# A third permanent buffer for raw weights, squares written elsewhere, and a new order, in a two-layer encoder on one core

## The chip, the cores and the metric

The kernel runs on one core of one Trainium2 chip, as one launch. The metric is the device time of that launch in microseconds. The time before is 1423.53 us, the median of three runs (1422.23 to 1426.47).

## The reference

The reference is a two-layer encoder trunk over 512 tokens of width 1024, all in float32. Each layer does

```
x = x + post_norm(mixer(pre_norm(x)))
x = x + post_norm(swiglu(pre_norm(x)))     # swiglu(h) = (silu(h @ w_gate) * (h @ w_up)) @ w_down
```

with RMS norms, `y = x / sqrt(mean(x*x) + 1e-6) * g`. The mixer of layer 0 is neighbourhood attention on an 8 x 64 grid (16 heads of 64, a window of 8 x 16 with a learned position bias); the mixer of layer 1 is a mixture of three dilated sliding-window attentions, (window, dilation) = (128, 1), (512, 4), (2048, 16), whose outputs are weighted by their softmax denominators. Each mixer ends in a projection by a 1024 x 1024 matrix. The channel mixer has a hidden width of 2816, that is 22 blocks of 128. The output is the stream x, 512 x 1024.

## The kernel before

The engines are called PE (TensorE, the matrix engine), DVE (VectorE), ACT (ScalarE), POOL (GpSimd) and SP (SyncE, which issues most transfers). Each works through its own row of instructions in order and waits on semaphores for the others.

**Products.** A float32 product is made of three products of a shorter format. Each operand is split into a high part, which ACT copies (L219), and a remainder, which DVE subtracts (L220); then `mm3` (L234 to L236) multiplies high by high, high by low and low by high into one bank of PSUM, the matrix engine's output memory. So every weight is loaded raw by a transfer, split by ACT and DVE into a slot of `wring`, and then multiplied. The large products of a layer are computed by a scheme with seven products of half-size blocks in place of eight; it needs sums of blocks of the weights. For gate, up and the mixers these sums are made on POOL and DVE from the raw weights in place (class `Seven`, L302 to L308). For down they are made beforehand in DRAM by POOL's transfers, some of which accumulate (tensor `wsum`, L749), and which stand between POOL's other instructions during the gate/up stage.

**Stages of a layer.** The mixer; then `out_proj`, which multiplies four blocks of 128 tokens (products 0 to 3, banks `yo`), applies the post-norm (`postnorm_half`, L506 and L507: a Square with a running sum on ACT, a multiply by the gain on DVE; `postnorm_sum`, L440 to L513), the next pre-norm (L438, L449), and turns the result by transposes on PE (`tr_o`, L465), which ACT and DVE empty into split operands (L456, L459); then `gate_up`, 22 units of one block of 128 hidden columns each, 84 matmuls 256 wide per unit; then `down`, seven products over the hidden blocks in pieces of two (matmuls 512 wide, banks `yd_pp` and `yd_s`), the last of which ends in the post-norm of token blocks 2 and 3 (`end`).

**Raw weights.** The pool `wpool` has a tag `raw` with two permanent buffers of 2 x 1024 floats per partition. In `gate_up` an arena `more` of six halves, a ring of three more buffers, stands beside them; the arena lies where operands of the mixer (`rxb`) were, so it can be loaded only after `out_proj` has ended. Of five units in a row the first two use permanent buffers (`f % 5 < 2`), the others the ring. `down` uses the same memory as a ring of ten halves, four of permanent buffers and six of the arena. Its first loads go to the permanent halves (in the profile `r_d`, issued at L779; gate/up weights there are `r_gu`, those in the arena `raw`).

**What sets the order.** Nothing is left to a scheduler: `TURNS`, a compressed table of numbers, holds for each engine the order in which the recorded instructions are to stand; `in_order` reads it and chains them.

**Scratch.** The program reserves memory in each partition for the descriptors of POOL's own transfers; by default 16 KB.

## Time and profile before

| | |
|---|---|
| median of the runs | 1423.53 us |
| profiled execution | 1423.35 us |
| span of its trace | 1421.6 us |
| mean granted clock of TensorE | 0.995 |
| busy: PE, DVE, ACT, POOL | 98%, 83%, 64%, 38% of the span |
| bytes moved | 253.21 MB, 178 GB/s |

The profile is of one execution; 1.75 us of it lie outside the span. A row of its timeline gives the start in us, the duration, the engine, the source line, the operation with its output and input tiles, how often it follows itself, and in brackets the idle time of that engine before the row and what ended it. "PEld" is the loading of weights into the matrix engine, which runs beside the matmuls. "SPq" and "POOLq" mark rows that issue transfers; such a row lasts as long as its queue was held, and the landing is given apart. Stretches list busy time by engine, the clock granted to TensorE (1.00 is full speed), the busy share of the DMA engines and what they moved. By stage: start 0 to 20, mixer of layer 0 to about 200, its `out_proj` to about 240, `gate_up` to 460, `down` to 560, the mixer of layer 1 to about 1050, `out_proj` to 1090, `gate_up` to 1310, `down` to the end.

### The profile page before, as it was taken

What the parts mean: (1) busy time and instruction counts of PE and PEld (TensorE: products, weight loads), DVE (VectorE), ACT (ScalarE), POOL (GpSimd) and SP (SyncE); (2) the same over time, 40 slices, a digit from 0 to 9 for tenths busy, and PEclk for the clock granted to TensorE, in tenths of its full rate; (3) what the DMA queues carried; (4) which work ended last, traced back from release to release, by engine and by line L of the source; (5) the groups of instructions that cost most, each with busy time, mean ns of one, the idle gap of its engine ahead of it and who ended that gap; (6) DMA issues with size and microseconds to landing.
All of it is one profiled execution on the core that took longest, in us unless ns stands there. A gap on an engine that the chain in (4) does not pass through costs nothing.

```text
span 1421.6 us, 27828 instructions
## 1 busy us (share of the span) xinstructions
PE 1387.5 (98%) x10714; PEld 1298.9 (91%) x10714; DVE 1181.7 (83%) x1891; ACT 914.0 (64%) x1853; POOL 541.5 (38%) x394
## 2 busy tenths in 40 slices
PE   8999999999999999999999999999999999999997
PEld 8989978999998888999999999999888999999886
DVE  7699969998887888997578887877748898897886
ACT  7489965555554767744467787888766555555674
...
GB/s 261 100 192 199 176 305 247 218 221 292 266 224 273 201 224 178 161 158 179 120 114 102 119 173 98 143 110 81 249 208 158 90 120 199 177 106 171 194 221 96
DMA packets 86645, 253.21 MB, mean 178 GB/s; under 512 B 19312, under 2 KB 31600, under 8 KB 84464
## 3 DMA queue, kind: packets, MB, share of 16 engines
...
## 4 chain that ended last, share of the span: by engine, by line
PE 78%; DVE 9%; ACT 6%; DMA 3%; issue 2%; POOL 1%; SPq 0%; POOLq 0%; DVEq 0%; ACTq 0%
PE gu L234 9%; PE gu L236 9%; PE gu L235 9%; PE pp_d L234 4%; PE pp_d L235 3%; PE pp_d L236 3%; DVE wring L220 3%; PE yd_s L235 3%; PE yd_s L234 3%; PE yd_s L236 3%; PE yd_pp L234 2%; PE yo L234 2%; PE yd_pp L235 2%; PE yd_pp L236 2%; PE yo L235 2%
## 5 line engine op out<-in xcount | busy, mean ns | idle before, releaser
L234 PE MATMUL gu<-rxa,wring 128*128 128x256 f32 x704 | 193.9, 280 | 0.7 <-DVE memc L715 0.3
L236 PE MATMUL gu<-rxa,wring 128*128 128x256 f32 x704 | 191.7, 278 | 1.9 <-DVE wring L220 1.9
L235 PE MATMUL gu<-rxa,wring 128*128 128x256 f32 x704 | 193.0, 277 | 0.0
L220 DVE TENSOR_TENSOR wring<-r_d,wring 128x1024 fp32r<-128x1024 f32 x112 | 142.6, 1280 | 38.9 <-ACT wring L219 38.5
L220 DVE TENSOR_TENSOR wring<-raw,wring 128x1024 fp32r<-128x1024 f32 (+1 forms) x120 | 152.0, 1276 | 16.6 <-ACT wring L219 15.3
L219 ACT ACTIVATE wring<-raw 128x1024 fp32r<-128x1024 f32 (+1 forms) x120 | 122.2, 1021 | 63.1 <-PE gu L235 36.5
L219 ACT ACTIVATE wring<-r_d 128x1024 fp32r<-128x1024 f32 x112 | 115.6, 1041 | 34.0 <-POOL r_d L304 6.4
L234 PEld LDWEIGHTS gu<-rxa,wring 128*128 128x128 f32 x704 | 131.6, 188 | 3.1 <-DVE mem L715 1.1
L236 PEld LDWEIGHTS gu<-rxa,wring 128*128 128x128 f32 x704 | 130.9, 188 | 3.0 <-DVE wring L220 2.5
L235 PEld LDWEIGHTS gu<-rxa,wring 128*128 128x128 f32 x704 | 132.2, 188 | 0.2
L234 PE MATMUL pp_d<-rxa,wring 128*128 128x256 f32 x384 | 107.4, 283 | 1.0 <-DVE mem L558 1.0
L442 POOL TENSOR_TENSOR rs_yd<-v_yd,consts 128x1 f32<-128x1 f32 x8 | 8.9, 1112 | 257.7 <-DVE v_yd L440 257.7
L235 PE MATMUL pp_d<-rxa,wring 128*128 128x256 f32 x384 | 106.1, 280 | 0.0
L236 PE MATMUL pp_d<-rxa,wring 128*128 128x256 f32 x384 | 105.0, 279 | 0.0
L235 PE MATMUL gu<-rxc,wring 128*128 128x256 f32 x352 | 98.1, 280 | 1.5 <-DVE rxc L459 1.5
L234 PE MATMUL gu<-rxc,wring 128*128 128x256 f32 x352 | 98.3, 282 | 0.5 <-ACT rxc L456 0.5
L236 PE MATMUL gu<-rxc,wring 128*128 128x256 f32 x352 | 97.8, 280 | 0.6 <-DVE wring L220 0.6
L219 ACT ACTIVATE rxc<-mem 128x512 fp32r<-128x512 f32 (+2 forms) x95 | 60.5, 644 | 51.3 <-PE yd_s L235 24.3
L302 POOL TENSOR_TENSOR raw<-raw 128x512 f32<-128x512 f32 x24 | 44.0, 1835 | 122.6 <-DVE wring L220 102.3
L219 ACT ACTIVATE wring<-r_gu 128x1024 fp32r<-128x1024 f32 x60 | 63.6, 1060 | 42.1 <-PE gu L235 19.3
L220 DVE TENSOR_TENSOR wring<-r_gu,wring 128x1024 fp32r<-128x1024 f32 x60 | 83.2, 1387 | 7.3 <-ACT wring L219 7.1
L220 DVE TENSOR_TENSOR rxc<-mem,rxc 128x512 fp32r<-128x512 f32 (+2 forms) x92 | 70.9, 777 | 14.1 <-ACT rxc L219 11.7
...
## 6 DMA issues: line engine op xcount, KB each, us to landing
wsum<-wd POOLq DMA_DIRECT2D x24, 1408.0 KB, 11.8
r_d<-dil_qk SPq DMA_DIRECT2D x48, 512.0 KB, 4.3
raw<-wg SPq DMA_DIRECT2D x24, 512.0 KB, 5.1
raw<-wu SPq DMA_DIRECT2D x24, 512.0 KB, 7.1
wsum<-wsum POOLq DMA_DIRECT2D x8, 1408.0 KB, 7.8
raw<-wsum SPq DMA_DIRECT2D x22, 512.0 KB, 4.4
r_gu<-wg SPq DMA_DIRECT2D x20, 512.0 KB, 5.5
r_gu<-wu SPq DMA_DIRECT2D x20, 512.0 KB, 5.9
```

The lines of the kernel that those rows point to most:

```text
L219: act.activation(h, src, AF.Copy)
L220: dve.tensor_sub(l, src, h.bitcast(F32))
L234: i = pe.matmul(o, s[0], m[0], start=start, stop=False, skip_group_check=True)
L235: pe.matmul(o, s[0], m[1], start=False, stop=False, skip_group_check=True)
L236: pe.matmul(o, s[1], m[0], start=False, stop=stop, skip_group_check=True)
L302: self.added = e[0].tensor_add(q[0], q[0], q[2])
L442: pool.tensor_tensor(r, v, mhalf, op=ALU.pow)
```

## The change

No operation is added or removed on any engine; what changes is where things stand, in memory and in each engine's row.

- The scratch for descriptors is 4 KB in place of 16. In the 12 KB set free lies a third permanent `raw` buffer (8 KB). In `gate_up`, three of six units in a row now use permanent buffers (`f % 6 < 3`), so units 0, 1, 2 may be loaded before the arena is there, where before 0 and 1 could, and units 18, 19 and 20 are the last in permanent buffers, where before 20 and 21 were. `down` has a ring of twelve halves in place of ten.
- The Square of a post-norm half no longer writes the place that the multiply then overwrites: in `out_proj` it writes the next block's buffer, in `end` a part of operands that are done with.
- In `down`'s last pass the last three pieces, not two, are kept until the others are done; they are then multiplied for token block 2 first and block 3 after.
- `TURNS` is new. Its text tells nothing; the rows of the engines show it below.

The diff, without `TURNS` (source lines after the table stand one line later than before, from `out_proj` on up to four):

```diff
@@ -210,7 +211,7 @@
 
     def load2(srcs, name, raw=None):
         if raw is None:
-            raw = tagged(wpool, [P, 2 * D], F32, "raw", f"r_{name}", 2)
+            raw = tagged(wpool, [P, 2 * D], F32, "raw", f"r_{name}", 3)
         for i in range(2):
             nc.sync.dma_start(raw[:, i * D:(i + 1) * D], srcs[i])
         return raw
@@ -501,9 +502,9 @@
             for i, v in ((D1, d1), (S2, s2), (S3, h1a), (S4, h1b)):
                 put(i, v)
 
-    def postnorm_half(hf, sq, y, g, name):
+    def postnorm_half(hf, sq, y, g, name, squares=None):
         m, s = small(f"ym{hf}_{name}"), slice(hf * 512, hf * 512 + 512)
-        act.activation(sq[:, s], y, AF.Square, scale=1.0 / 32.0, accum_out=m)
+        act.activation(sq[:, s] if squares is None else squares, y, AF.Square, scale=1.0 / 32.0, accum_out=m)
         dve.tensor_mul(sq[:, s], y, g[:, s])
         return m
 
@@ -512,8 +513,8 @@
         for s in ([slice(0, 512), slice(512, 1024)] if halves else [ALL]):
             dve.scalar_tensor_tensor(x[:, s], sq[:, s], r, x[:, s], op0=ALU.mult, op1=ALU.add)
 
-    def postnorm(sq, y, g, x, name):
-        postnorm_sum(sq, [postnorm_half(hf, sq, y[hf], g, name) for hf in range(2)], x, name)
+    def postnorm(sq, y, g, x, name, squares=(None, None)):
+        postnorm_sum(sq, [postnorm_half(hf, sq, y[hf], g, name, squares[hf]) for hf in range(2)], x, name)
 
     def v_quarter(vt, srcs, name, raw=None):
         u = units2(srcs, name, raw=raw, at=0)
@@ -646,7 +647,7 @@
         g1 = gain(gains[0], a["g_mix_post"][layer])
         g2 = gain(gains[1], a["g_ffn_pre"][layer])
         us = [u for k in range(0, KD, 2) for u in units2(w[k:k + 2], f"wo{k}_{layer}", us[k:k + 2])]
-        hs = {}
+        hs = {0: next(rhn)}
 
         def product(t):
             y = [bank(("pp", "pp", "s", "s", "pp", "o", "pp", "pp")[2 * t + hf], f"yo{layer}_{t}_{hf}")
@@ -658,9 +659,12 @@
             return y
 
         def post(t, y):
-            x, hs[t] = next(rbig), next(rhn)
+            x = next(rbig)
             load_x(x, t)
-            postnorm(hs[t], y, g1, x, f"o{layer}_{t}")
+            if t < NT - 1:
+                hs[t + 1] = next(rhn)
+            postnorm(hs[t], y, g1, x, f"o{layer}_{t}",
+                     (hs[t + 1][:, :512], hs[t + 1][:, 512:]) if t < NT - 1 else (None, None))
             nc.sync.dma_start(spill[2 * layer][t], x)
             xs_[t] = x
 
@@ -700,7 +704,7 @@
         def unit_of(f):
             if f in units or f >= FT:
                 return units.get(f)
-            raw = load2((wg[layer, f], wu[layer, f]), f"gu{layer}_{f}", None if f % 5 < 2 else next(raws))
+            raw = load2((wg[layer, f], wu[layer, f]), f"gu{layer}_{f}", None if f % 6 < 3 else next(raws))
             b, g = bank(("s", "s", "pp", "o", "pp", "pp")[f % 6], f"gu{layer}_{f}"), next(g_)
 
             def sink(n, left, other):
@@ -761,7 +765,7 @@
         x1a, x1b, x2a, x2b = (hm[:, i * QF:(i + 1) * QF] for i in range(4))
         pieces = [slice(2 * i, min(2 * i + 2, FT // 2)) for i in range(FT // 4 + 1)]
         last = len(pieces) - 1
-        raws = [tagged(wpool, [P, 2 * D], F32, "raw", f"r_d{layer}{i}", 2) for i in range(2)]
+        raws = [tagged(wpool, [P, 2 * D], F32, "raw", f"r_d{layer}{i}", 3) for i in range(3)]
         raws = [r[:, i * D:i * D + D] for i in range(2) for r in raws]
         raw_ = cycle(raws + [more[:, i * D:i * D + D] for i in range(6)])
         ga, gb, ua, ub = (a["wd"][layer, i] for i in range(4))
@@ -858,7 +862,7 @@
             kept = []
             for i, w in enumerate(loaded(uab if n == 0 else every)):
                 ops = operands2(xp((x1a, x2b)[n], i), w, f"{nm}{('s3', 'x2b')[n]}_{i}")
-                if i > last - 2:
+                if i > last - (3 if n else 2):
                     kept.append(ops)
                 else:
                     prod(left, ops)
@@ -877,7 +881,7 @@
                 prod(left, ops, False, (m,))
 
         def end():
-            m0 = [postnorm_half(0, hs[t], left[t - 2], gp, f"d{layer}_{t}") for t in (2, 3)]
+            m0 = [postnorm_half(0, hs[t], left[t - 2], gp, f"d{layer}_{t}", xp(x2b, t - 2)) for t in (2, 3)]
             for t in (2, 3):
                 postnorm_sum(hs[t], (m0[t - 2], ms[t - 2]), xts[t], f"d{layer}_{t}", layer == 1 and t == NT - 1)
                 out_of(t)
@@ -1395,7 +1399,7 @@
               .reshape(2, 4, P, 2 * QF),
     }
     arrays = {n: np.ascontiguousarray(v) for n, v in arrays.items()}
-    nc = bacc.Bacc("TRN2", target_bir_lowering=False, num_devices=1)
+    nc = bacc.Bacc("TRN2", target_bir_lowering=False, num_devices=1, dynamic_dma_scratch_size=4096)
     aps = {n: nc.dram_tensor(n, v.shape, mybir.dt.from_np(v.dtype), kind="ExternalInput").ap()
            for n, v in arrays.items()}
     out = nc.dram_tensor("out", (NT, P, D), F32, kind="ExternalOutput").ap()
```

What the new order does is shown at three places. A number behind a name tells apart tiles of one name; it differs between the two programs.

The first place is the end of `gate_up` in layer 0, on PE: `yd_pp` is the first product of `down`, `gu_18` to `gu_21` are units of gate/up. Before:

```order
L234 MATMUL gu_21_4872<-rxa,wring 128x256
L235 MATMUL gu_21_4872<-rxa,wring 128x256
L236 MATMUL gu_21_4872<-rxa,wring 128x256
L234 MATMUL yd_pp_5193<-wring,rxc 128x512
L234 MATMUL yd_pp_5194<-wring,rxc 128x512
L234 MATMUL gu_20_4762<-rxa,wring 128x256
```

and now:

```order
L235 MATMUL yd_pp_5195<-wring,rxc 128x512
L235 MATMUL yd_pp_5196<-wring,rxc 128x512
L235 MATMUL gu_19_4655<-rxa,rxc 128x256
L236 MATMUL gu_19_4655<-rxa,rxc 128x256
L237 MATMUL gu_19_4655<-rxa,rxc 128x256
```

The first matmuls of `down` stood among the last two units, with 48 matmuls of gate/up behind them; they now stand among units 18 to 20, with 132 behind them. What feeds them is a split on DVE. Its row from the last split of unit 18 (`r_gu_18`) to the first of the down weights (`r_d`) is now:

```order
L221 TENSOR_TENSOR wring<-r_gu_18_4542,wring 128x1024
L309 TENSOR_TENSOR r_gu_19_4652<-r_gu_19_4652 128x512
L816 TENSOR_TENSOR mem<-mem 128x512
L221 TENSOR_TENSOR wring<-r_gu_19_4652,wring 128x1024 x2
L717 TENSOR_TENSOR memc_2767<-memc_2767,gu_18_4545 128x256
L221 TENSOR_TENSOR vbig<-r_gu_20_4762,vbig 128x512
L305 TENSOR_TENSOR r_gu_20_4762<-r_gu_20_4762 128x512
L309 TENSOR_TENSOR r_gu_20_4762<-r_gu_20_4762 128x512
L723 TENSOR_TENSOR mem<-memc_2767,mem 128x2x256
L719 TENSOR_TENSOR memc_2767<-mem,gu_18_4545 128x256
L221 TENSOR_TENSOR wring<-r_gu_20_4762,wring 128x1024
```

with five more rows (a sum, a memset and three splits of 512) before `wring<-r_d`. Before, the buffer came free with unit 20, and from its last split to that of `r_d` 15 rows of the same kinds stood between. On SP, six loads into the arena stood right ahead of the first load of `r_d`; now there are three.

The second place is the end of `out_proj` in layer 1, on PE. `yo_3` is the product of token block 3, `tr_o_0` and `tr_o_1` are the transposes of blocks 0 and 1. Before:

```order
L465 MATMUL tr_o_0_0_11762<-ident,mem 128x128 x4
L236 MATMUL yo_3_0_11856<-rxb_5993,rxa 128x512
L234 MATMUL yo_3_1_11857<-rxb_5993,rxa 128x512
L235 MATMUL yo_3_1_11857<-rxb_5993,rxa 128x512
L236 MATMUL yo_3_1_11857<-rxb_5993,rxa 128x512
L465 MATMUL tr_o_0_1_11769<-ident,mem 128x128 x4
L465 MATMUL tr_o_1_0_11776<-ident,mem 128x128 x4
L465 MATMUL tr_o_1_1_11783<-ident,mem 128x128 x4
L234 MATMUL gu_0_12014<-rxc,wring 128x256
```

and now, at the first of them and at the third:

```order
L236 MATMUL yo_3_1_11860<-vbig,rxa 128x512
L466 MATMUL tr_o_0_0_11765<-ident,mem 128x128 x4
L466 MATMUL tr_o_0_1_11772<-ident,mem 128x128 x2
L237 MATMUL yo_3_1_11860<-wm_11591,rxa 128x512
L235 MATMUL yo_3_0_11859<-rxa 128x512
L236 MATMUL yo_3_0_11859<-rxa 128x512
```

```order
L235 MATMUL yo_3_0_11859<-rxb_5996,rxa 128x512
L236 MATMUL yo_3_0_11859<-rxb_5996,rxa 128x512
L237 MATMUL yo_3_0_11859<-rxb_5996,rxa 128x512
L466 MATMUL tr_o_1_0_11779<-ident,mem 128x128 x4
L466 MATMUL tr_o_0_1_11772<-ident,mem 128x128 x2
L236 MATMUL yo_3_1_11860<-rxb_5996,rxa 128x512
```

Four products stood between the first group and the three that end the stage; now 25 products follow the first group and 14 the group `tr_o_1_0`, and the last of these groups stands behind 14 matmuls of units 2 and 0. On DVE the norms of blocks 0, 1 and 2 are now taken one after the other; before, block 1's came first, and half of block 2's (`yo_2_0`) before block 0's:

```order
L507 TENSOR_TENSOR mem<-yo_1_1_11677,mem 128x512
L507 TENSOR_TENSOR mem<-yo_1_0_11676,mem 128x512
L513 SCALAR_TENSOR_TENSOR mem<-mem,consts 128x1024
L507 TENSOR_TENSOR mem<-yo_2_0_11790,mem 128x512
L507 TENSOR_TENSOR mem<-yo_0_0_11626,mem 128x512
```

In layer 0's `out_proj` the first transpose moves up likewise: it stood at the end of product 3 and now stands behind the first four matmuls of it.

The third place is the end of the program, on DVE, with what each row waits for. Before:

```order
L507 TENSOR_TENSOR mem<-yd_s_14435,mem 128x512 [waits Activation_49]
L440 TENSOR_SCALAR v_yd_2_15193<-ym_d_2_15187,ym_d_2_15162 128x1
L507 TENSOR_TENSOR memc_12005<-yd_s_14436,mem 128x512 [waits Activation_49]
L440 TENSOR_SCALAR v_yd_3_15199<-ym_d_3_15190,ym_d_3_15165 128x1
L513 SCALAR_TENSOR_TENSOR mem<-mem,rs_yd_2_15195 128x1024 [waits DMAHW3_49,Pool_49]
```

and now:

```order
L508 TENSOR_TENSOR mem<-yd_s_14440,mem 128x512 [waits Activation_49]
L441 TENSOR_SCALAR v_yd_2_15199<-ym_d_2_15193,ym_d_2_15156 128x1
L508 TENSOR_TENSOR memc_12008<-yd_s_14441,mem 128x512 [waits Activation_49]
L441 TENSOR_SCALAR v_yd_3_15205<-ym_d_3_15196,ym_d_3_15159 128x1
L514 SCALAR_TENSOR_TENSOR mem<-mem,rs_yd_2_15201 128x1024 [waits DMAHW3_49,Pool_49]
```

`L507`/`L508` is the multiply of a post-norm half. Its order and its wait for ScalarE ("Activation") are the same in both.

More of the change, by code (lines that the diff above doesn't have):

```diff
@@ new lines @@
+    "SDA~+gP1tnFl?4s!r*cQOq^J1A&W$RZZPrHd+yEq02j0zln>wBbg*B-E&bsK`|`>-B4B~>3j@Bt1I*0K+@7&GWT5_4ZscdcO$SlY_yq=6-;U1W"
+    "`ybQ>@WV#&G%B#>;BJ8#2X_SY?#RJ)16fn8HCijW{+WQAzbHs5ZV~(q==`g;kqBB_d;Z+*>8QZ-=g;YsgGYGx!Gj0=`+bWm4vLoF0QA4Ab~}~k"
+    "&$85PZ4qq<9CqS4zd&!_05e|$-1XC^W(eq+xa{j8u;5@QxaPp~NRcyXgS<fWqxw-1(`L&77<_%b;O^z+<#h+k20yoOIG<-smyB8{R#kA-;(`NI"
+    "I5*fH3<g{^&sX!@WiCics}%yHkxOCIQC`BC5SjJeu_8_-8JC#tqsUpnyZ7$h1NYn`sp7Pk=QpF9q*>6YRk5CB)XmL*R{Z%F`H-$NXz|jeOP3A~"
+    "4lW5Oym+ZY-p=ms{?1Nv;R4i5G5y5U{6$GUp(-u$G%#(97~;+Yny$EeJ*+g85>~yt)LrZ@bRA$3imL(j`w)e^fgV>!Q`|^e0}p|xcK+uN&I`E5"
@@ new lines @@
+    "NhF>D6RY*O)$#_kHXzB+qybmOaAE~6X)#4qhsUGOu`c;QMAu93j&B4X@3cI~nQHr*B^OlN(mKS*)fxtQs@TxseA7kRMJ<hL!bhm1L=T)5c3@>N"
+    "ocD1R$*4Vuc^C(A8_OI+fOG^(<$(e__G6akN*KYUJr?s)V5>(gxhJ?#%@QNIP!0iw$|)I%n1B;};)2u<R1&HgexxE54x=Gthk6}MAtQ}fK+k~Z"
+    "$?_^Q#)p}%kZ1d;q}&R(_ByVVlV}I?rq)JRa0_1LyI?WIVo=<RQP81O66xHjyft9j6Z4lClSS>5IDsDb((iV25#ZC*?vPF3@(5<c9H>r5LA;dN"
+    "Li59LK?TgvqrQ}M=uG*{Us7Qp7RMwj!CA>#TI{9yQ7BJoh=)0zGS_7prsK8Sag2f?8#Z%(CMDA*L>$`RH$9qm(lzDzm|Z{%U?|_8g?M2aMNCM="
+    "Mk4pV1@31-S9FQ!;_DEc5G%XjBYxMXp(G9Kfpi@<fEk}}@Vr(#Bk+9?x45|DdkM5b2Es*hvL?Wr5fo`cQO<W!pxW&&`Uv<DCX%pn>U2oQN@XBp"
```

97 lines of the change are left out of this document (44 added, 53 removed).

## The prediction

> **What bounds the kernel now.** I read the page's overview first, then the chain of waits, then TensorE's own waits, and last the stretches in which those waits lie.
>
> ```profile
> PE 1387.5 (98%) x10714; PEld 1298.9 (91%) x10714; DVE 1181.7 (83%) x1891; ACT 914.0 (64%) x1853; POOL 541.5 (38%) x394
> PE 78%; DVE 9%; ACT 6%; DMA 3%; issue 2%; POOL 1%; SPq 0%; POOLq 0%; DVEq 0%; ACTq 0%
> 300.00:340.00 40.00, 40.00 (x352) 40.00 (x351) 37.40 (x47) 19.35 (x34) 20.41 (x16) 1.00 0.91 290
> 470.00:510.00 40.00, 40.00 (x178) 33.09 (x177) 36.10 (x48) 25.78 (x38) 0.00 (x0) 1.00 0.67 217
> ```
>
> TensorE (PE) is busy 98% of the span of 1421.6 us, so some 34 us are idle. The two stretches (columns: PE, PEld, DVE, ACT, POOL busy, granted clock, DMA share, GB/s) give its undisturbed pace: 40/352 = 0.114 us for a matmul 256 wide in gate_up, 40/178 = 0.225 us for one 512 wide in down. The change adds and removes no matmul, so it can gain only where TensorE runs below that pace. I looked for those places with TensorE's waits:
>
> ```profile
> PE yd_pp L234 <- ACT wring L219: 2.9, 1, 2.9
> PE tr_a L465 <- DVE rxa L459: 2.7, 1, 2.7
> PE gu L236 <- DVE wring L220: 2.6, 4, 0.7
> PE pp_d L234 <- DVE pp_d L292: 2.1, 4, 1.4
> PE tr_o L465 <- DVE rxc L459: 1.0, 2, 0.5
> ```
>
> No one wait dominates; the largest single one is the first product of layer 0's down.
>
> **Third raw buffer and the first down weights: -3.0.** This is the transition from gate_up to down in layer 0, by stretches of 5 us, with the instructions in it:
>
> ```profile
> 420.00:425.00 5.00, 5.00 (x46) 5.00 (x46) 5.00 (x5) 2.83 (x6) 5.00 (x4) 1.00 0.01 3
> 435.00:440.00 5.00, 5.00 (x45) 4.88 (x44) 5.00 (x7) 2.72 (x6) 0.00 (x0) 1.00 1.07 252
> 445.00:450.00 5.00, 4.89 (x42) 4.69 (x41) 4.97 (x9) 2.87 (x5) 0.00 (x0) 1.00 1.05 261
> 450.00:455.00 5.00, 3.18 (x27) 2.97 (x26) 2.95 (x5) 0.36 (x2) 0.00 (x0) 1.00 1.00 283
> 455.00:460.00 5.00, 3.88 (x18) 3.61 (x19) 1.23 (x1) 1.33 (x2) 0.00 (x0) 0.66 0.62 215
> 442.40 1.21 DVE L220 TENSOR_TENSOR wring<-r_gu,wring 128x1024 fp32r<-128x1024 f32 x1
> 443.64 14.51 SPq L779 DMA_DIRECT2D r_d<-wd  x5
> 455.01 1.06 ACT L219 ACTIVATE wring<-r_d 128x1024 fp32r<-128x1024 f32 x1 [4.65 <-DMA r_d<-wd]
> 456.12 1.22 PE L234 MATMUL yd_pp<-wring,rxc 128*128 128x512 f32 x2 [2.94 <-ACT wring L219]
> 458.63 0.55 PE L235 MATMUL yd_pp<-wring,rxc 128*128 128x512 f32 x1
> 459.01 0.39 PE L236 MATMUL yd_pp<-wring,rxc 128*128 128x512 f32 x1
> ```
>
> From 450 to 460, 27 + 18 = 45 matmuls ran, four of them wide: 41 x 0.114 + 4 x 0.225 = 5.6 us of work in 10 us. With 0.3 us in 445 to 450 (42 instead of 45) the loss is 4.7 us. Its cause reads upwards: the load of the first down weights could be issued only at 443.64, when unit 20's last split (442.40 + 1.21) had freed the permanent buffer, and it landed 11.4 us later, while the DMA engines, empty in 420 to 425 (0.01), were full (1.07, 1.05). What filled them:
>
> ```profile
> wsum<-wd POOLq DMA_DIRECT2D x2, 1408.0 KB, 17.6
> raw<-wd SPq DMA_DIRECT2D x5, 512.0 KB, 7.2
> 431.85 2.37 POOL L749 DMA_DIRECT2D wsum<-wd  x2
> r_d<-wd SPq DMA_DIRECT2D x14, 512.0 KB, 4.5
> ```
>
> The first two are this stretch's issues (425 to 462; the last number is the median landing in us), the last is the whole kernel's. With three buffers the unit that frees the first down buffer is 18, not 20. In the new order unit 18's last split stands 14 VectorE instructions ahead of the first down split. At the start-to-start of such rows (splits of 1024 about 1.13 us, of 512 about 0.6, of 256 about 0.34) these make 10 us, against 9 us for the 15 of the old order, so the lead alone buys only 1 us of the wait of 2.94. The rest hangs on the landing. It lies between 4.5 us (the kernel's median) and 11.4 us (as now): the last two accumulations into wsum are still issued some 10 us ahead of it, but three loads of SP's queue stand right ahead of it, one of them half as large, where six do now. At 10 - 1.1 (ScalarE's copy, 455.01 to 456.10) = 8.9 us or less the wait is gone; the nearest row is the 7.2 us of the loads issued into the same full stretch. **I take -3.0, two thirds of the way, with bounds 0 and -4.7.** What is late next: the third buffer's first down piece, which unit 20 frees 13 VectorE rows, again some 9 us, before its split. TensorE then still has products of unit 21 to run beside it, which hide it; uncovered, it would cost the old 2.94 over again.
>
> **New order at out_proj to gate_up of layer 1: -2.5.**
>
> ```profile
> 1080.00:1085.00 5.00, 3.97 (x24) 2.98 (x22) 4.50 (x9) 2.75 (x7) 2.56 (x3) 1.00 0.22 51
> 1085.00:1090.00 5.00, 3.98 (x22) 3.78 (x22) 5.00 (x7) 3.96 (x6) 4.90 (x4) 0.70 0.98 370
> 1079.28 1.28 DVE L449 SCALAR_TENSOR_TENSOR mem<-mem,consts 128x1024 f32<-128x1024 f32 x1
> 1081.30 0.60 PE L465 MATMUL tr_o<-ident,mem 128*128 128x128 f32 x4
> 1081.65 0.48 PE L236 MATMUL yo<-rxb,rxa 128*128 128x512 f32 x1
> 1083.80 0.66 PE L465 MATMUL tr_o<-ident,mem 128*128 128x128 f32 x4 [0.53 <-DVE rxc L459]
> 1084.95 0.66 PE L465 MATMUL tr_o<-ident,mem 128*128 128x128 f32 x4 [0.50 <-DVE rxc L459]
> 1086.87 0.48 PE L235 MATMUL gu<-rxc,wring 128*128 128x256 f32 x1 [1.02 <-DVE rxc L459]
> ```
>
> Here 46 matmuls took 10 us: 9 wide products (2.0), 19 transposes at 0.35 us for four (1.7; 1081.30 to 1081.65) and 18 narrow ones (2.1) are worth 5.8, so 4.2 us are lost. Three groups of transposes stand back to back behind the last product, each waiting for VectorE to empty the one before. The new order puts the first of them 25 products (25 x 0.225 = 5.6 us) ahead of that product's end and block 1's first 14 ahead (3.2 us), and lets VectorE take the blocks in the order 0, 1, 2, where it now does half of block 2 before finishing block 0. Then only one group and the first matmuls of gate_up remain exposed; a third raw unit, loaded early, gives six more matmuls that can run first. Bounds 0 (the same waits elsewhere) and -4.2; I take about three fifths, since VectorE is busy 4.5 and 5.0 of 5 us here and still has the last block's work to do.
>
> The granted clock falls to 0.70 here after waits of 1.02 us at most, and to 0.66 in 455 to 460 after one of 2.94. The Trainium skill ("TensorE: Matmul & The Clock Gate", Part 1: The HAM clock gate) has the clock halve after an idle window of about 3.4 us. The trace does not keep to that figure: shorter waits were enough. By that rule this place would cost its waits alone, 2 us of the 4.2, and this term would be about -1.2 in place of -2.5 (1420.3 in all); the sum goes by the rows.
>
> **New order at the same place in layer 0: +1.0.**
>
> ```profile
> 221.36 2.32 DVE L449 SCALAR_TENSOR_TENSOR mem<-mem,consts 128x1024 f32<-128x1024 f32 x1
> 230.87 0.60 PE L465 MATMUL tr_o<-ident,mem 128*128 128x128 f32 x4
> 235.00:240.00 5.00, 4.10 (x34) 3.65 (x32) 4.76 (x7) 2.75 (x6) 4.92 (x5) 1.00 0.95 290
> ```
>
> The first transpose, at 230.87 now, is moved up by some 6.5 us of TensorE's row, to 224.4; the VectorE row that feeds it, ended at 223.68, gets about 2 us of other work ahead of it, to 225.7. That is a new wait of 1.3 to 1.4 us in the middle of out_proj. Against that, part of the 0.9 us lost in 235 to 240 may go: +1.0, with bounds -0.9 (no new wait) and +2.5 (VectorE 3 us late).
>
> **The rest of the order: 0.** Every engine's row is permuted nearly everywhere, which deals anew the waits for tr_a, gu and pp_d in the list above (2.7 + 2.6 + 2.1 = 7.4 us) and smaller ones. I find rows of VectorE and ScalarE that go earlier and rows that go later, by 1 to 3 us, and no side to prefer: 0, with about half of the 7.4 to either side, -3.7 and +3.7, as ends. In down there is nothing to win (40.00 of 40.00).
>
> **Squares written elsewhere: 0.** The edit gives the Square (ACT) and the multiply (VectorE) of a post-norm half different targets. The end shows them:
>
> ```profile
> 1412.99 0.39 PE L236 MATMUL yd_s<-wring,rxc 128*128 128x512 f32 x1
> 1413.48 0.60 ACT L506 ACTIVATE memc<-yd_s 128x512 f32<-128x512 f32 x1 [1.41 <-PE yd_s L236]
> 1414.20 0.69 DVE L507 TENSOR_TENSOR memc<-yd_s,mem 128x512 f32<-128x512 f32 x1 [1.29 <-ACT memc L506]
> 1415.16 1.45 POOL L442 TENSOR_TENSOR rs_yd<-v_yd,consts 128x1 f32<-128x1 f32 x1 [1.55 <-DVE v_yd L440]
> 1416.64 1.42 DVE L513 SCALAR_TENSOR_TENSOR mem<-memc,rs_yd,mem 128x512 f32<-128x512 f32 x2 [0.44 <-POOL rs_yd L442]
> ```
>
> VectorE waits until the Square is over, and 0.72 us (1413.48 to 1414.20) lie on the path to the end. But both still read the same bank of products, and in the instructions of the changed kernel the multiply keeps its wait for ScalarE. So 0; -0.7 if the wait only looks the same.
> The Trainium skill says why such a wait stays ("PSUM — Partial Sum Buffer", PSUM bank collisions raise a hardware error): two engines must not touch one bank at once, so accesses are guarded by bank. The rows agree so far as they show no overlap. By that rule the edit is worth 0.
>
> **One more piece kept in down's last pass: 0.** It gives block 2 its last sum 6 x 0.225 = 1.35 us sooner; but the end hangs on block 3 through the rows just shown, and the order of VectorE's last seven rows is the old one.
>
> **Scratch of 4 KB: 0.** Only POOL's own transfers use it (wsum 32, keys and values 14). If the smaller ring made POOL wait until one transfer has landed before the next is issued, POOL would be held up to 17.6 us at a pair like that of 431.85. It is 38% busy, and idle for 19.6 of 40 us in the gate_up row above, which hides it. Uncovered, a raw sum late by 5 us would stop TensorE for as much.
>
> **Sum.** -3.0 - 2.5 + 1.0 = -4.5. The profiled execution took 1423.35 us (span 1421.6), 0.2 below the median of the runs; the median less 4.5 gives **1419.0 us**.
>
> **Rivals.**
> *The wait for the first down weights stays* (no change to tell). The first down product now stands 132 narrow matmuls before gate_up's end on TensorE, not 48, so it wants its weights 84 x 0.114 = 9.6 us earlier in TensorE's row. If the load still takes 11 us, about 2 us of waiting and the slow clock stay, at this piece or at the third buffer's: -1 - 2.5 + 1.0 = -2.5, 1421.0. For it: a lead of only 1 us more, and accumulations as near as before. Against: the landing rows.
> *VectorE's splits come late in gate_up* (slower). A unit is 84 narrow matmuls, 9.6 us; VectorE is idle 40 - 37.40 = 2.6 us in 4.2 units, 0.6 us a unit. A unit whose split stands later than now by more than that makes TensorE wait for the rest. The rows that go later go by 1 to 3 us, so about 2 - 0.6 = 1.4 us for each unit that is hit. Three of the 44 units eat the gain; from the seventh on the kernel is slower than can be put down to measurement: 7 x 1.4 = 9.8, 1428.8. For it: the little slack, and an order in which a third unit's splits stand among the first two's. Against: only four such waits now, 2.6 us together, and VectorE's work is the same in sum.
> *The order clears other waits as well* (faster): half of the 7.4, and the new wait in layer 0 does not come, 1419.0 - 3.7 - 1.0 = 1414.3. For it: in layer 1 the new row is plainly the better sorted one. Against: nothing that I can point to in the other places.
>
> **How the numbers follow.** Chances: forecast 0.38, the wait stays 0.22, late splits 0.20, other waits too 0.20. A measurement here can tell about 0.3%, 4.3 us, from no change, and the forecast lies just beyond that bound: 0.23 of its 0.38 count as faster, with the 0.20 of the last case and 0.02 of the second: faster 0.45, same 0.35, slower 0.20. The forecast's own range is 1416 to 1422, from its terms' bounds; to hold 8 in 10 it must reach past 1414.3 below and into the slower case above: 1411 to 1427.
>
> **What would show it.** Right: the wait at the first yd_pp of layer 0 under 1 us and the clock 1.00 there; its load landing in under 9 us; the counterpart of 1080 to 1090 with 60 or more matmuls in 10 us; a new wait of about 1.4 us before the first tr_o of layer 0; Square and multiply still one after the other at the end. Wrong: yd_pp still waiting for r_d, more or longer waits for VectorE's splits within gate_up, or POOL rows of wsum that last many microseconds.

## The result

| | before | changed |
|---|---|---|
| median of the runs shown with the result | 1425.70 us (6) | 1416.35 us (6) |
| lowest to highest | 1422.23 to 1428.25 | 1414.93 to 1417.13 |
| profiled execution | 1423.35 us | 1416.33 us |
| span of its trace | 1421.6 us | 1414.6 us |

The ratio is 0.9934 (95%: 0.9918 to 0.9950): the change is faster by 9.4 us in medians and by 7.0 in the profiled executions. The forecast was 1419.0 in a range of 1411 to 1427. Two runs of this study, one of the kernel before (2775.15 us) and one with 18 added warming products (3534.15 us), lie far from all others and are left out of every median and ratio.

The page of the changed kernel shows the engines about as busy as before, VectorE with 85% of the span instead of 83% (busy time, share of the span, instructions):

```profile
PE 1387.7 (98%) x10714; PEld 1301.1 (92%) x10714; DVE 1195.9 (85%) x1891; ACT 912.3 (64%) x1853; POOL 542.8 (38%) x394
```

Among TensorE's longer waits (total, number, longest) there is no yd_pp and no tr_o any more. The longest is at the start of the kernel; those within gate_up are shorter than before:

```profile
PE tr_a L466 <- DVE v_a L439: 2.5, 1, 2.5
PE gu L237 <- DVE wring L221: 0.9, 2, 0.7
```

These are the two places on which the prediction rested, in the changed kernel: first the end of gate_up of layer 0, then out_proj of layer 1 (the counterpart of 1080 to 1090).

```profile
450.00:455.00 5.00, 5.00 (x43) 4.88 (x42) 3.65 (x6) 1.85 (x3) 0.00 (x0) 1.00 0.48 189
455.00:460.00 5.00, 5.00 (x41) 4.81 (x40) 4.12 (x6) 2.89 (x5) 0.00 (x0) 1.00 0.65 222
1080.00:1085.00 5.00, 5.00 (x36) 4.64 (x35) 3.46 (x7) 2.07 (x6) 3.64 (x5) 1.00 0.37 94
1085.00:1090.00 5.00, 5.00 (x46) 5.00 (x45) 4.56 (x6) 3.27 (x6) 2.47 (x3) 1.00 1.01 401
```

TensorE is busy throughout and runs 84 and 82 matmuls where before 45 and 46 ran. The rows behind the first place read:

```profile
430.43 1.21 DVE L221 TENSOR_TENSOR wring<-r_gu,wring 128x1024 fp32r<-128x1024 f32 x1
431.70 0.33 SPq L783 DMA_DIRECT2D r_d<-wd  x1
443.13 1.06 ACT L220 ACTIVATE wring<-r_d 128x1024 fp32r<-128x1024 f32 x1 [2.02 <-PE gu L236]
```

and the issue of 431.70 in the view of transfers, whose last number is the landing:

```profile
r_d<-wd SPq DMA_DIRECT2D x1, 512.0 KB, 9.1
```

Unit 18's last split ends at 431.6, the first down load is issued at 431.70 and lands 9.1 us later, at 440.8. ScalarE takes the piece at 443.13, and what it waited for is TensorE, not the load, which had landed 2.3 us earlier.

**Where the 7.0 us lie.** I counted TensorE's loss piece by piece: the time that passed, less the matmuls in it at their undisturbed durations (0.1135 us for 256 columns, 0.225 for 512, 0.0875 for a transpose). Before lost 79.2 us in all, the changed kernel 72.2. At equal work done, the differences are:

| place | change of the loss, us |
|---|---|
| start, to about 32 us | +1.9 |
| mixer of layer 0, to about 184 us | -4.1 |
| end of its attention, about 184 to 208 us | +3.5 |
| out_proj of layer 0 | -0.2 |
| end of gate_up, start of down of layer 0 | -4.6 (5.3 to 0.7) |
| start of layer 1's mixer, about 560 to 600 us | +1.6 |
| out_proj to gate_up of layer 1 | -4.9 (7.3 to 2.4) |
| everything else | -0.2 |

So two places bring 9.5 us, and the other places give back 2.5. The stretches of the first three places, of the kernel before:

```profile
5.00:20.00 15.00, 10.85 (x74) 9.90 (x74) 11.33 (x16) 12.75 (x24) 3.16 (x5) 0.89 0.87 303
51.00:186.00 135.00, 130.83 (x1064) 121.83 (x1065) 117.91 (x288) 110.02 (x272) 73.71 (x79) 1.00 0.61 188
186.00:208.00 22.00, 22.00 (x122) 17.13 (x118) 11.92 (x32) 14.65 (x34) 2.22 (x5) 1.00 1.01 360
```

and of the changed one:

```profile
5.00:20.00 15.00, 10.19 (x56) 9.22 (x56) 10.84 (x15) 12.02 (x22) 2.22 (x4) 0.77 0.89 325
51.00:186.00 135.00, 132.76 (x1091) 124.26 (x1090) 122.38 (x292) 112.81 (x276) 75.22 (x80) 1.00 0.61 191
186.00:208.00 22.00, 19.71 (x103) 15.25 (x102) 12.94 (x32) 13.71 (x33) 3.20 (x5) 1.00 0.87 312
```

TensorE is busier in the mixer, less so at the end of attention, and the clock at the start is 0.77 instead of 0.89.

### The profile page after: what moved, and what is told of

It reads as the page before. It is cut to its first block, busy times and chain, and to the rows that moved or that the text cites. A ratio compares the mean times of both kernels' runs of the same rounds, so it can differ in the third digit from the quotient of the medians.

```text
span 1414.6 us, 27833 instructions
## 1 busy us (share of the span) xinstructions
PE 1387.7 (98%) x10714; PEld 1301.1 (92%) x10714; DVE 1195.9 (85%) x1891; ACT 912.3 (64%) x1853; POOL 542.8 (38%) x394
## 5 line engine op out<-in xcount | busy, mean ns | idle before, releaser
L221 DVE TENSOR_TENSOR wring<-r_d,wring 128x1024 fp32r<-128x1024 f32 (+1 forms) x124 | 157.3, 1274 | 43.9 <-ACT wring L220 41.0
L220 ACT ACTIVATE wring<-r_d 128x1024 fp32r<-128x1024 f32 (+1 forms) x124 | 126.4, 1023 | 61.4 <-PE pp_d L236 31.6
L220 ACT ACTIVATE wring<-raw 128x1024 fp32r<-128x1024 f32 x96 | 99.5, 1039 | 58.6 <-PE gu L236 41.0
L221 DVE TENSOR_TENSOR wring<-raw,wring 128x1024 fp32r<-128x1024 f32 x96 | 126.8, 1327 | 11.9 <-ACT wring L220 9.3
L220 ACT ACTIVATE wring<-r_gu 128x1024 fp32r<-128x1024 f32 x72 | 76.0, 1061 | 55.6 <-PE gu L236 31.5
L221 DVE TENSOR_TENSOR wring<-r_gu,wring 128x1024 fp32r<-128x1024 f32 x72 | 102.7, 1434 | 7.5 <-ACT wring L220 7.1
L443 POOL TENSOR_TENSOR rs_yd<-v_yd,consts 128x1 f32<-128x1 f32 x8 | 9.9, 1234 | 253.5 <-DVE v_yd L441 253.5
L236 PE MATMUL gu<-rxc,wring 128*128 128x256 f32 x352 | 96.9, 279 | 0.3 <-DVE rxc L460 0.3
L235 PE MATMUL gu<-rxc,wring 128*128 128x256 f32 x352 | 96.2, 279 | 0.5 <-ACT rxc L457 0.5
L237 PE MATMUL gu<-rxc,wring 128*128 128x256 f32 x352 | 96.7, 278 | 0.0
L303 POOL TENSOR_TENSOR r_gu<-r_gu 128x512 f32<-128x512 f32 x24 | 40.7, 1695 | 127.3 <-DVE wring L221 55.2
```

Source lines behind the costliest of these rows:

```text
L220: act.activation(h, src, AF.Copy)
L221: dve.tensor_sub(l, src, h.bitcast(F32))
L235: i = pe.matmul(o, s[0], m[0], start=start, stop=False, skip_group_check=True)
L236: pe.matmul(o, s[0], m[1], start=False, stop=False, skip_group_check=True)
L237: pe.matmul(o, s[1], m[0], start=False, stop=stop, skip_group_check=True)
L303: self.added = e[0].tensor_add(q[0], q[0], q[2])
```

## The experiments

Times are medians; a ratio is to the kernel before, which ran beside each group. Over all its runs in this study the kernel before has a median of 1424.74 us (66 runs, 1421.67 to 1430.99).

**The scratch alone.** The kernel before, with

```diff
-    nc = bacc.Bacc("TRN2", target_bir_lowering=False, num_devices=1)
+    nc = bacc.Bacc("TRN2", target_bir_lowering=False, num_devices=1, dynamic_dma_scratch_size=4096)
```

> The kernel before with one edit: 4 KB of scratch for descriptors instead of 16, nothing placed in the memory set free. My theory: nothing waits for room in the ring, so the time is that of before within 2 us, and POOL's rows that issue wsum last 0.5 to 1.6 us as before. Rival (the ring is too small): POOL is held until a transfer has landed, its wsum rows last many microseconds, the kernel is slower by 3 us or more, and the change has gained that much more elsewhere.

Measured: 1424.43 us, ratio 0.9996 (0.9979 to 1.0012). The group of GpSimd's rows that issue the transfers into wsum has 24.1 us for 24 issues, and the wait of yd_pp is 2.9 us, as before. The smaller scratch costs nothing that these runs can tell (the interval is -3.0 to +1.7 us), and the rival's 3 us or more are not there.

**The squares put back.** The changed kernel, with

```diff
-        act.activation(sq[:, s] if squares is None else squares, y, AF.Square, scale=1.0 / 32.0, accum_out=m)
+        act.activation(sq[:, s], y, AF.Square, scale=1.0 / 32.0, accum_out=m)
```

> The changed kernel, but the Square of each post-norm half writes where the multiply then writes, as before. My theory: both wait for each other by the bank they read anyway, so within 2 us of the changed kernel (0.993 of before), and at the end the multiply still starts 0.72 us after the Square. Rival (the edit removed a wait): slower than the changed kernel by 0.7 us at the end and by up to 8 halves x 0.7 = 5.6 us with out_proj.

Measured: 1416.57 us, 0.9944 (0.9925 to 0.9963), beside the changed kernel's 1416.35. At the end the Square starts at 1405.29 and the multiply at 1406.01, 0.72 us later, as in the kernel before and the changed one. Putting the squares back costs nothing that these runs can tell.

**The old order at out_proj of layer 1.** The kernel just told of, with the rows of all engines between about 1035 and 1103 us in the order of the kernel before.

> The kernel of squares_undone, with the rows of all five engines put back into the old order in one stretch only, from about 1035 to 1103 us (out_proj of layer 1 and the first units of gate_up); third buffer, scratch and the rest of the order as in the changed kernel. By the traces TensorE lost 4.9 us less in that stretch after the change. My theory: that is the order there alone, so slower than squares_undone by 4 to 5 us, with the three waits at the transposes back. Rival (the third buffer, with unit 2 loaded early, did it): at most 1 us slower.

Measured: 1418.89 us, 0.9959 (0.9947 to 0.9971): 2.3 us more than with the new order there, and the loss of that place is 2.3 us larger as well. The three old waits are back to the hundredth:

```profile
1083.41 0.66 PE L464 MATMUL tr_o<-ident,mem 128*128 128x128 f32 x4 [0.53 <-DVE rxc L458]
1084.57 0.66 PE L464 MATMUL tr_o<-ident,mem 128*128 128x128 f32 x4 [0.50 <-DVE rxc L458]
1086.48 0.39 PE L234 MATMUL gu<-rxc,wring 128*128 128x256 f32 x1 [1.02 <-DVE rxc L458]
```

But the clock behind them is 1.00 in this kernel's stretch,

```profile
1085.00:1090.00 5.00, 3.98 (x35) 3.77 (x33) 5.00 (x6) 4.11 (x7) 4.50 (x4) 1.00 0.96 368
```

where before had 0.70 and the scratch experiment 0.72. I expected 4 to 5 us and measured 2.3: the order's own share is the waits, and the slow clock is something that the same waits do not always bring. That question is taken up below.

**The first down piece into unit 19's buffer.** The changed kernel, with

```diff
-        raws = [r[:, i * D:i * D + D] for i in range(2) for r in raws]
+        raws = [r[:, i * D:i * D + D] for i in range(2) for r in (raws[1], raws[0], raws[2])]
```

> The changed kernel, but the first piece of down goes into the buffer that unit 19 frees, the second into that of unit 18. In the trace of the changed kernel unit 18's last split ends at 431.6 and unit 19's at 435.8 us, and the load landed 9.1 us after its issue with 2.3 us to spare. My theory (the time from the freed buffer to the first split is what counts): the load is issued 4.2 us later, lands 1.9 us late, and layer 0's first product of down waits 1.5 to 2.5 us again, with some slow clock; slower than the changed kernel by 1.5 to 3.5 us. Rival (the load landed late only because of the queue ahead of it): it then lands sooner, and nothing changes.

Measured: 1415.67 us, 0.9937 (0.9916 to 0.9957), no change; but the edit did not do what it was meant to. The buffers are handed out in the order of the first loads, so only the names changed places: the first load was again issued behind unit 18's last split (431.92 against 431.70). The run is a repeat of the changed kernel and says nothing of the lead.

**The accumulations out of the way.** The kernel before, with GpSimd's row changed in one place, so that the pair is issued at 537.83 us instead of 431.85:

```diff
 TENSOR_TENSOR r_gu0_21<-r_gu0_21 128x512
-DMA wsum1<-wd 128x2x1408 x2
 TENSOR_TENSOR rs_yd0_0<-v_yd0_0,consts 128x1
+DMA wsum1<-wd 128x2x1408 x2
```

> The kernel before, with one thing moved: GpSimd's last two accumulations into layer 0's summed down weights (the pair at 431.85, 2 x 1.4 MB) stand behind the first post-norm power of down in GpSimd's row, so they are issued some 70 us later and are out of the way of the first down load. Two buffers, the old order and the old lead stay. Theory A (landing): the load at 443.64 took 11.4 us because those accumulations share the DMA engines with it; it now lands in 5 us (the kernel's median is 4.5), which is under the 452.0 - 443.6 = 8.4 us at which TensorE does not have to wait, so the wait of 2.94 at the first yd_pp and the clock of 0.66 behind it go: -4.6 us, about 1420. Theory B (the lead alone, or SP's own six loads of 0.5 MB right ahead): landing 9 to 11 us, wait 2 to 3 us, no change in time (-0.5 to 0). Side question, the clock in layer 1: the waits before gate_up of layer 1 (0.53, 0.50, 1.02) stay as they are but come some 4.6 us sooner under A. If the waits bring the slow clock, the stretch of 10 us there shows 0.70 to 0.75 again; if its place in time does, 0.9 to 1.00.

Measured: 1419.70 us, 0.9962 (0.9949 to 0.9975). Its stretches:

```profile
450.00:455.00 5.00, 5.00 (x43) 4.92 (x42) 5.00 (x9) 2.80 (x5) 0.00 (x0) 1.00 0.10 12
455.00:460.00 5.00, 5.00 (x41) 4.83 (x40) 2.13 (x4) 1.35 (x4) 0.00 (x0) 1.00 0.98 360
```

its first down load and ScalarE's copy of it, and that load's landing:

```profile
445.13 11.27 SPq L777 DMA_DIRECT2D r_d<-wd  x5
451.73 1.06 ACT L217 ACTIVATE wring<-r_d 128x1024 fp32r<-128x1024 f32 x1
```

```profile
r_d<-wd SPq DMA_DIRECT2D x1, 512.0 KB, 3.6
```

With two buffers, the old order and the old lead, the load lands in 3.6 us instead of 11.3, ScalarE no longer waits for it, TensorE has no wait for yd_pp, and the loss there falls from 5.3 to 0.8 us: theory A. The two accumulations of 1.4 MB account for the late landing in the kernel before. The side question: the three waits before gate_up of layer 1 came 1.6 us sooner in this execution and the clock behind them was 0.66.

**The end of attention in the old order.** The changed kernel, with the old order from 180 to 212 us. On GpSimd the piece reaches to 219 us, since only there both orders have done the same instructions.

> The changed kernel, with the order of the kernel before on every engine from 180 to 212 us (end of layer 0's attention), and nothing else. The trace of the changed kernel loses 3.5 us more there than the kernel before (new waits of TensorE: s for VectorE's mn 1.16, ta for GpSimd's mem 1.12 and 0.51). Theory (losses are local): -3.5 us, about 1412.9, and the three waits gone. Rival (the stretch only takes back what was gained in 51 to 186 us, and a later stretch takes it back again): 0 to -1 us.

Measured: 1421.62 us, 0.9978 (0.9969 to 0.9987): 5.3 us slower. The three waits are gone, but 4.2 us of waiting and two slow stretches come in out_proj. GpSimd's row there with TensorE's wait in this kernel, and GpSimd's row in the changed one:

```profile
216.21 0.57 POOL L441 TENSOR_TENSOR consts<-consts 128x1 f32<-128x1 f32 x1 [21.61 <-DVE consts L439]
216.76 1.28 POOL L301 TENSOR_TENSOR r_gu<-r_gu 128x512 f32<-128x512 f32 x1
218.12 2.87 POOL L302 TENSOR_TENSOR r_gu<-r_gu 128x512 f32<-128x512 f32 x1
...
223.00 1.01 POOL L441 TENSOR_TENSOR consts<-consts 128x1 f32<-128x1 f32 x1
228.99 0.47 PE L464 MATMUL tr_o<-ident,mem 128*128 128x128 f32 x1 [4.16 <-DVE consts L437]
```

```profile
209.65 1.30 POOL L303 TENSOR_TENSOR r_gu<-r_gu 128x512 f32<-128x512 f32 x1 [13.23 <-DMA r_gu<-wu]
211.03 1.30 POOL L304 TENSOR_TENSOR r_gu<-r_gu 128x512 f32<-128x512 f32 x1
...
215.03 0.57 POOL L443 TENSOR_TENSOR consts<-consts 128x1 f32<-128x1 f32 x1 [1.54 <-DVE consts L441]
...
216.84 0.55 POOL L443 TENSOR_TENSOR consts<-consts 128x1 f32<-128x1 f32 x1
```

The new order makes the first unit's sums on GpSimd while it idles before the first norm's power (a small instruction on 128 x 1 values, L443, at 215.03). In the mixture they stand behind that power (216.21), so the second power comes at 223.00 instead of 216.84, VectorE waits for it, and TensorE for VectorE. Counted as loss, the stretch itself gains 3.5 us and loses 3.1 at its front (a wait of 1.8 for pp_n), which is the rival's 0 to -1; what neither theory had is the 6.5 us lost behind it. This stretch of the order can't be exchanged alone.

**A mixture of what looked best.** The changed kernel, with the old order in 0 to 28 and 180 to 212 us, and the swap told of next.

> The changed kernel with the old order in 0 to 28 us (there the trace of the changed kernel loses 1.9 us more than the one before) and in 180 to 212 us (3.5 us more), and with VectorE's row of the tail swapped (0.9). If the three losses are local and add up: 1416.35 - 1.9 - 3.5 - 0.9 = 1410.1 us. Rival (each shift of a stretch deals the waits behind it anew, and the start is given back): 1413 to 1415.

Measured: 1421.04 us, 0.9967 (0.9955 to 0.9979), 4.7 us slower than the changed kernel; neither expected value came. The trace loses 7.1 us in out_proj of layer 0, the place of the experiment before.

**The last rows of VectorE.** In the changed kernel GpSimd's last power takes 1.45 us beside a VectorE addition, where the one before it, alone, takes 0.55. The edit, in VectorE's row:

```diff
 TENSOR_SCALAR v_yd1_2<-ym0_d1_2,ym1_d1_2 128x1
+SCALAR_TENSOR_TENSOR mem<-mem,rs_yd1_2 128x1024
 TENSOR_TENSOR memc1<-yd1_s1,mem 128x512
 TENSOR_SCALAR v_yd1_3<-ym0_d1_3,ym1_d1_3 128x1
-SCALAR_TENSOR_TENSOR mem<-mem,rs_yd1_2 128x1024
```

> The changed kernel, with one row of VectorE moved in its last ten: the scaled addition of block 2 (second half) goes ahead of block 3's last multiply by g, where VectorE now idles 2.64 us, instead of behind it. Theory: GpSimd's last power (1.45 us beside that addition, 0.55 where it runs alone) then runs alone, and VectorE is free for block 3's first addition as soon as the power is done: -0.9 us, a span of 1413.7 against 1414.6, everything before the last 10 us unchanged. Rival: the power takes 1.45 us whatever runs beside it: -0.3 to 0 us.

Measured: 1415.92 us, 0.9939 (0.9928 to 0.9951), a span of 1413.7. The rows at the end:

```profile
1405.34 1.28 DVE L512 SCALAR_TENSOR_TENSOR mem<-mem,rs_yd 128x1024 f32<-128x1024 f32 x1 [0.73 <-POOL rs_yd L441]
1408.22 0.55 POOL L441 TENSOR_TENSOR rs_yd<-v_yd,consts 128x1 f32<-128x1 f32 x1 [2.91 <-DVE v_yd L439]
1408.80 1.41 DVE L512 SCALAR_TENSOR_TENSOR mem<-memc,rs_yd,mem 128x512 f32<-128x512 f32 x2 [0.73 <-POOL rs_yd L441]
```

From the last matmul's start to the end of the span it is 7.7 us (1406.06 to 1413.7) instead of 8.6 (1405.97 to 1414.6): -0.9, as expected. In the medians 0.4 us is less than these runs can tell.

**The third unit's six products.** The changed kernel, with six products of unit 2 moved behind the next transposes in out_proj of layer 1:

```diff
-MATMUL gu1_2<-rxc,wring 128x256 x6
 MATMUL gu1_0<-rxc,wring 128x256
...
 MATMUL tr_o1_2_3<-ident,mem 128x128 x4
+MATMUL gu1_2<-rxc,wring 128x256 x6
```

> The changed kernel, with the six products of the third raw unit that stand between the groups of transposes before gate_up of layer 1 (six of the row at 1086.19 to 1087.0) moved behind the next group. My prediction counted them as part of the gain there, as products that can run while VectorE empties the transposes' bank. If they cover a wait: a new wait of 0.5 to 0.9 us before that group and +0.5 to +0.9 in this place. Rival (the earlier start of the transposes alone does it): no wait over 0.2 us, +0 to +0.2.

Measured: 1416.04 us, 0.9941 (0.9924 to 0.9958), and TensorE is busy 5.00 of 5.00 us in every stretch from 1070 to 1095: no wait. The six are among the 14 matmuls that run from 1082.02 to 1083.66 in the changed kernel, ahead of transposes, and not those at 1086.19 that the expectation names. They cover nothing; the rest of the new order there does it, the earlier transposes and VectorE's order of the norms, which no run tells apart.

**What makes the slow clock.** With the granted clock read in stretches of 2 us, the slow stretches of one execution all begin at the same phase of a period of 3.41 us, to more places 3.4133 (before: 11.80, 455.53 and 1087.00, that is 1.56 us after a whole number of periods; adds_late: 13.29, 1085.08, 1412.76, that is 3.05) and each lasts one such period or several. So I cut the traces into these periods. Of the kernel before:

```profile
452.12:455.53 3.41, 1.06 (x9) 0.85 (x8) 0.83 (x2) 0.52 (x1) 0.00 (x0) 1.00 0.98 325
455.53:458.94 3.41, 2.82 (x10) 2.64 (x11) 1.23 (x1) 0.81 (x2) 0.00 (x0) 0.50 0.46 151
1083.59:1087.00 3.41, 1.68 (x11) 1.24 (x12) 2.95 (x7) 2.38 (x6) 3.33 (x4) 1.00 0.90 310
1087.00:1090.41 3.41, 3.41 (x17) 3.41 (x18) 3.41 (x3) 2.67 (x4) 2.90 (x2) 0.50 1.01 346
```

of l1_out_old, where the same waits fall differently into the periods:

```profile
1084.04:1087.45 3.41, 1.89 (x15) 1.66 (x15) 3.41 (x7) 2.79 (x4) 3.33 (x5) 1.00 0.88 353
1087.45:1090.86 3.41, 3.41 (x33) 3.41 (x32) 3.41 (x4) 2.44 (x5) 2.19 (x2) 1.00 1.01 380
```

and of the changed kernel and six_later, whose rows are the same at this place:

```profile
565.64:569.05 3.41, 1.69 (x13) 1.41 (x13) 3.41 (x6) 3.41 (x8) 0.55 (x1) 1.00 0.12 47
569.05:572.46 3.41, 3.41 (x19) 3.41 (x18) 3.41 (x7) 2.63 (x6) 1.23 (x2) 0.50 0.72 226
```

```profile
565.92:569.33 3.41, 1.90 (x14) 1.69 (x15) 3.41 (x6) 3.41 (x7) 0.55 (x1) 1.00 0.14 53
569.33:572.74 3.41, 3.41 (x32) 3.41 (x31) 3.41 (x6) 3.39 (x6) 1.50 (x2) 1.00 0.72 203
```

A period in which TensorE is busy 1.06, 1.68 or 1.69 of 3.41 us is followed by one at half clock (17 and 19 matmuls where there is work, instead of 32); with 1.89 or 1.90 none follows. Counted from the matmuls of the fourteen traces of this study, from 4.5 us on and up to the last matmul, 25 periods at full clock were followed by a slow one, and TensorE was busy in them for 0.50 of the time at most; over 5600 were not, and it was busy for 0.51 at least. At the end of the kernels the rule has one exception: the period of l1_out_old in which the last matmul ends, 1408.31 to 1411.72, has 1.54 us busy (0.45), and the clock behind it is still 1.00. So the rule describes these traces; what exactly is counted stays open. A slow period costs 1.7 us where TensorE has work, and at half clock it takes more to get out: those with TensorE busy for 0.82 of the time or less were followed by another, from 0.83 on by none. To test the rule, idle time was filled with products that nobody needs.

In the kernel before, 11 products ahead of the first yd_pp of layer 0:

```diff
+        for _ in range(11 if layer == 0 else 0):
+            pe.matmul(right[0], rxa[:, 0:P], rxa[:, 0:512], start=True, stop=True, skip_group_check=True)
         for i, w in enumerate(loaded(gb)):
             prod(right, operands2(xp(x1b, i), w, f"{nm}p2_{i}"), i == 0)
```

> The kernel before, with 11 products of 512 columns more, whose results are thrown away, in TensorE's row right ahead of the first product of layer 0's down, where TensorE idles 2.94 us (11 x 0.225 = 2.5 us; TensorE computes that much more than it needs). Rule to be tested, read from the ten traces so far: all slow stretches of one execution begin at the same phase of a period of 3.41 us and last 3.4 us, and one follows each period in which TensorE is busy for half or less (busy 0.50 at most ahead of the slow ones, 0.51 at least ahead of the others). By it the clock stays 1.00 in 450 to 460 us although the load still lands late: the loss of that place falls from 5.3 us by 1.7, and, the phase being another in every execution, the median by about 0.87 x 1.7 = 1.5 us. Rival (the wait for the load as such, or the DMA traffic, brings the slow clock): 0.66 to 0.88 again, and no gain.

```profile
450.00:455.00 5.00, 5.00 (x43) 4.87 (x42) 4.33 (x8) 1.61 (x3) 0.00 (x0) 1.00 1.06 275
455.00:460.00 5.00, 4.36 (x25) 3.51 (x24) 1.23 (x1) 1.33 (x2) 0.00 (x0) 1.00 0.61 222
```

The wait for the load (2.94 before) is down to what the products leave of it:

```profile
PE yd_pp L232 <- ACT wring L217: 0.6, 1, 0.6
```

The clock stays 1.00 beside the same late load and equally busy DMA engines (1.06 and 0.61, before 1.00 and 0.62), so here neither of these brought the slow clock. The loss, the 2.5 us of idle products counted in, falls by 1.2 us there (1.7 expected). Since the products also cut the wait itself to 0.6 us, this run can't tell the rule from one about the length of a single wait; the three short waits of layer 1 do, with a slow period behind them in the kernel before and none in l1_out_old. The mean granted clock, which every run gives, has a median of 0.997 here and of 0.995 in the runs of the kernel before; one slow period takes 3.41 x 0.5 / 1420 = 0.0012. The time is 1424.34 us, 0.9995 (0.9987 to 1.0004): the 1.5 us that I expected lie within that interval, but the runs don't show them.

In the kernel of the swap, 18 more warming products in TensorE's gap between the first two groups of transposes:

```diff
-    for i in range(30):
+    for i in range(48):
         pe.matmul(warm[:, i % 2 * 256:i % 2 * 256 + 256], rxc[:, 2304:2432], rxc[:, 2304:2560], start=True, stop=True)
```

> The kernel of tail_swap, with 18 more of the warming products of the first row (256 columns, 0.113 us each at full clock, results thrown away) behind the first 8 transposes, where TensorE idles 2.5 us (9.1 to 11.7 us). In the traces so far the clock is at half from about 12 us on for one to three periods of 3.41 us (three in tail_swap). By the rule (a period with TensorE busy for half or less brings a slow one) the period around 9 to 12 us is now about 0.8 busy and no slow one follows: clock 1.00 from 8 us on. Each slow period takes up to 1.7 us, part of which is the splits' pace anyhow (VectorE and ScalarE 2.00 of 2.00 us in most of 12 to 18): -1.5 to -3 us against tail_swap, about 1413.5. Rival (the splits set the pace of the start): the clock is 1.00 and the time the same (0 to -0.5). Rival (the clock at the start comes from elsewhere): half clock again, and 0 to +0.5.

and the same with 10:

> As warm_gap, but with 10 warming products instead of 18 in the gap of 2.5 us (1.1 us of 2.5). By the rule half of a period is enough: the gap's idle time falls to about 1.4 us of a period of 3.41, so the clock at the start stays 1.00 with ten as with eighteen, and the time is warm_gap's (1415 within 0.5) or a little less, since fewer products stand ahead of the next transposes. If the clock needs an uninterrupted TensorE, a slow period of 3.4 us comes back at about 12 us: +0.5 to +1.5.

The periods at the start, of tail_swap, and of the kernels with 18 and with 10 products:

```profile
7.48:10.89 3.41, 1.09 (x8) 0.85 (x8) 1.76 (x4) 3.21 (x6) 0.55 (x1) 1.00 0.98 356
10.89:14.30 3.41, 2.29 (x9) 1.75 (x9) 3.20 (x6) 3.39 (x8) 0.55 (x1) 0.50 0.83 328
```

```profile
7.22:10.63 3.41, 3.18 (x27) 2.98 (x27) 1.81 (x3) 3.03 (x6) 0.55 (x1) 1.00 0.99 368
10.63:14.04 3.41, 1.96 (x14) 1.32 (x12) 3.20 (x6) 3.41 (x8) 0.55 (x1) 1.00 0.88 345
```

```profile
11.71:15.12 3.41, 1.55 (x10) 1.11 (x11) 3.22 (x4) 3.41 (x7) 0.55 (x1) 1.00 0.74 257
15.12:18.54 3.42, 3.42 (x17) 3.42 (x18) 2.82 (x5) 2.78 (x5) 0.55 (x1) 0.50 0.96 351
```

With 18 the start has no slow period (tail_swap had three, from 10.89 to 21.1). With 10 the gap itself brings none either, but the next wait (1.55 us for wring) fell whole into one period, with 1.55 us busy, and one slow period followed: my expectation that none would come was wrong, the rule is not. The losses up to 32 us, the idle products counted in, are 13.5 us in tail_swap, 12.5 in the changed kernel and 11.0 with 18 products. The times are 1415.07 us, 0.9929 (0.9916 to 0.9942), and 1415.61, 0.9936 (0.9924 to 0.9948). Both lie under the changed kernel, and the version with swap and 18 products has the lowest median of all, but by less than the runs can tell.

## Why the prediction was right, and where not

- **Third buffer and first down weights, -3.0: the mechanism held, the size was 4.6.** The lead came out at 11.4 us (431.70 to 443.13) where I had 10 from counting rows, and the landing at 9.1. I took two thirds because the landing was unknown; with 2.3 us to spare the whole wait of 2.94 went, and the slow period behind it (1.7). The step "the lead alone buys only 1 us" was mis-sized: without its wait TensorE would have wanted the copy at 455.01 - 2.94 = 452.07, so the old lead was 8.4 us (from 443.64), not 9, and the new one is 3.0 longer. By these rows, as an estimate, the longer lead alone would just have covered the wait, and the earlier landing alone would have left 0.7 us of it. The landing missed my sign of being right, "under 9 us", by 0.1. Also wrong in the working: the accumulations do not stand some 10 us ahead of the load but, in the changed kernel's trace, 7.7 and 5.4 (424.05 and 426.29). That they were what held the load up in the kernel before is shown by adds_late. That the lead, with a landing of 9.1, is what removes the wait in the changed kernel follows from its rows; the experiment on the lead failed, and the third buffer and the new order were not tried apart.
- **Order at out_proj of layer 1, -2.5: right in sign and mechanism, mis-sized; 4.9 measured.** The waits are worth 2.3 us (l1_out_old). Most of the other 2.6 is the slow period that followed in the profiled execution of before (1.7), which I had not priced apart from the waits. The step "a third raw unit gives six more matmuls that can run first" failed: moved away, they uncover no wait.
- **Out_proj of layer 0, +1.0: failed, -0.2 measured.** The new wait of 1.3 to 1.4 us did not come. I had the VectorE row that feeds the first transpose end at 225.7 and the transpose at 224.4; the row ended at 223.6 (222.31 for 1.28), and the transpose ran at 225.59 without a wait. I moved one row by what stands ahead of it and left the other engine where it was; and I kept the row's old length of 2.32 us, which it had while GpSimd made sums beside it.
- **The rest of the order, 0: +2.7 measured,** inside its ends of 3.7 to either side. 1.6 to 1.9 each are slow periods at the start and at 569 us; the mixer's -4.1 and +3.5 nearly cancel.
- **Squares 0, scratch 0: right** within what the runs can tell, each by its own run. **The kept piece, 0:** not tried alone; the end is 8.6 us behind the last matmul's start in both kernels (1412.99 to 1421.6, 1405.97 to 1414.6).
- **The rivals.** The wait for the load did not stay, and the splits did not come late: gu waits for wring 0.9 us in two places, against 2.6 in four. Other waits did not clear on balance.
- **The total came partly by luck.** The terms missed by -1.6, -2.4, -1.2 and +2.7 us; the last took back half of the others, and the sum missed the profiled difference by 2.5.
- **The reading of the clock was incomplete.** I wrote that shorter waits than 3.4 us were enough to slow the clock, against the Trainium skill ("TensorE: Matmul & The Clock Gate", Part 1: The HAM clock gate). They were, but not each by itself: the same three waits of layer 1 had a slow period behind them in the kernel before and none in l1_out_old. That part has a window of 3413 ns that runs free of the kernel, and the traces agree: the slow stretches of one execution keep to multiples of it within 0.03 us. What they don't bear out is that the window must be idle throughout: half idle was enough, and several waits in one window added up.
- **Medians.** The forecast was made against a median of three runs, 1423.53. Over 66 runs the kernel before has 1424.74, so the change is worth some 8 us in medians against 7.0 in the profiled pair. The mean clock does not explain the rest (0.995 and 0.994 in the profiled executions), and it stays open.
